# The gated half's LayerNorm as two fused VectorE steps, its splits moved into the gate's projection

## Chip, cores and metric

The kernel runs on one core of one Trainium2 chip. The metric is the device time of one execution in microseconds (us). The time before is 1013.77 us, the median of 3 runs (1012.42 to 1014.16).

## What is computed

One layer of a streaming encoder on x with 512 tokens of 1024 channels. The part that matters here is the token mixer: three branches read the same modulated input h, each is projected to 1024 channels, and the three are merged by sigmoid gates. The change lies in the third branch, a spatial gate.

```python
def _sgu(uv, g_sg, b_sg, w_s, b_s):
    uv = jax.nn.gelu(uv, approximate=False)
    u, v = jnp.split(uv, 2, axis=-1)
    v = _layer_norm(v) * g_sg + b_sg            # over the 1024 channels of a token
    v = v.reshape(B, nb, SG_BLOCK, SG_GROUPS, SG_GW)      # blocks of 128 tokens, 8 groups of 128 channels
    z = jnp.einsum('gts,bnsgc->bntgc', ws, v) + b_s[:, :, None]
    return u * z.reshape(B, S, SG_WIDTH)

    merged = gates[:, :, 0] * y_a + gates[:, :, 1] * y_b + gates[:, :, 2] * y_c
    return merged @ w_o
```

Six rows of modulation (shift, scale and gate for each sub-layer) come from a product of the condition vector with w_ada. After the mixer come a residual LayerNorm, a gated MLP with a short convolution, and a second LayerNorm.

## The kernel before

All matrix products are made from f32 data split in two: a high part (rounded to the type that TensorE takes, a copy on ScalarE) and a low part (value minus high part, on VectorE). `mm3` issues three matmuls for each product. Weights come in chunks of 128 x 1024: `load` brings one from memory on SyncE's queue (3 buffers), `wsplit` makes the high part on ScalarE (L90) and the low part on VectorE (L91), with two buffers for each part. `chunk` takes the chunks in the order of a written plan and splits one chunk ahead of use.

The 512 tokens are four tiles (TT = 4) of 128. The stage around the change runs in this order:

- `uv_half(2)` and `uv_half(3)` project the two halves of v (512 channels each). A half takes four weight chunks (q = 0 to 3) of 24 matmuls, and at its end a Gelu on ScalarE (L803) writes one tile for each token tile: `v0[t]` and `v1[t]`. `uv_half` can take a hook, called after each chunk.
- Four row tiles are loaded: `gsg` and `bsg`, gain and offset of v's LayerNorm, in two halves, each copied to all partitions.
- Eight merges of the second branch (m = 0 to 7): a gate (for m = 4 to 7 projected here by 24 matmuls and put through tanh at L278; the first four were made earlier), a projection of 24 matmuls (`py`), its product with the gate on VectorE (L295) and the sum on GpSimd (L298, POOL in the profile). Beside each merge runs `ada_piece(1, m)`: two loads `adar` of w_ada and two accumulations on VectorE (L678, L680). The LayerNorm of v (`v_norm`) stands beside merges 0 to 3, a whole token tile each: statistics on VectorE, inverse root on GpSimd (`power`: L113, L116; L125 makes the shift), scale and shift on VectorE (L816), gain on VectorE (L819), offset on GpSimd (L820). The splits of the normalised v (`v_split`, L829 and L830), two groups of channels each, stand beside merges 4 to 7. `ada_cols` then turns the accumulated row into columns (`pmc`).
- `sg_weights`, then `uv_half(0)` and `uv_half(1)` project u; beside the second, `z_step` makes the spatial products, which read v's splits.
- Three more groups of modulation accumulate in the same way (`ada_piece(2, m)` belongs to the merges of the third branch).

The program's lines give an order of precedence, but a planner fixes the order of instructions on each engine when the kernel is built, from its own costs and from when inputs and buffers are ready in its model. An instruction can therefore be issued ahead of lines above it. On the chip each engine then runs its list in order. Tiles with one tag share a fixed number of buffers: `pt` has eight, and holds `gsg`, `bsg`, the row tiles of the first residual gate (`gttb`), the two accumulators of a modulation row and its loads `adar`; `act` has 48.

Of the kernel before, what the change touches and what calls it, by code (L numbers as in the profile page):

```python
# [8 lines left out]
F32 = mybir.dt.float32  # L9
# [3 lines left out]
ALU = mybir.AluOpType  # L13
AX = mybir.AxisListType

P = 128
# [3 lines left out]
TT = 4  # L20
# [6 lines left out]
LN_EPS = 1e-5  # L27
# [23 lines left out]
def trunk(ctx: ExitStack, tc: tile.TileContext, A, out):  # L51
    nc = tc.nc

    const = ctx.enter_context(tc.tile_pool(name="const", bufs=1))
    sb = ctx.enter_context(tc.tile_pool(name="sb", bufs=1))
    wp = ctx.enter_context(tc.tile_pool(name="wp", bufs=2))
    sm = ctx.enter_context(tc.tile_pool(name="sm", bufs=4))
    pp = ctx.enter_context(tc.tile_pool(name="pp", bufs=8, space=bass.MemoryType.PSUM))

    def ps(name):  # L60
        return pp.tile([P, 512], F32, name=name, tag="ps")

    def act_t(name, dt=F32R):
        return sb.tile([P, 512], dt, name=name, tag="act", bufs=48)
# [13 lines left out]
    def f(ap):  # L78
        return ap.bitcast(F32)
# [16 lines left out]
    def mm3(o, wh, wl, xh, xl, start, stop):  # L96
        nc.tensor.matmul(o, wh, xl, start=start, stop=False)  # L97
        nc.tensor.matmul(o, wl, xh, start=False, stop=False)  # L98
        nc.tensor.matmul(o, wh, xh, start=False, stop=stop)  # L99
# [11 lines left out]
    def power(dst, src, scale, eps, n):  # L111
        t = sm.tile([P, 8], F32, name="pw", tag="pw")
        nc.gpsimd.tensor_scalar(  # L113
            out=t[:, :n], in0=src, scalar1=scale, scalar2=eps, op0=ALU.mult, op1=ALU.add
        )
        nc.gpsimd.tensor_tensor(out=dst, in0=t[:, :n], in1=neghalf[:, :n], op=ALU.pow)  # L116
# [3 lines left out]
    def ln_finish(st):  # L120
        mv = sm.tile([P, 2], F32, name="mv", tag="mv")
        a = nc.vector.bn_aggr(out=mv, in_=st.rearrange("p a b -> p (a b)"))  # L122
        rs = sm.tile([P, 2], F32, name="rs", tag="rs")
        power(rs[:, 0:1], mv[:, 1:2], 1.0, LN_EPS, 1)
        b = nc.gpsimd.tensor_scalar(  # L125
            out=rs[:, 1:2], in0=mv[:, 0:1], scalar1=rs[:, 0:1], scalar2=-1.0, op0=ALU.mult, op1=ALU.mult
        )
        last[:] = [a.ins, b.ins]
        return rs

    def ln_stats(halves):
        st = sm.tile([P, 2, 6], F32, name="st", tag="st")
        for i, hv in enumerate(halves):
            nc.vector.bn_stats(out=st[:, i, :], in_=hv)
        return ln_finish(st)

    def row_tiles(r, alloc, name):
        ts = []
        for n in range(2):
            t = alloc(f"{name}{n}", F32)  # L140
            nc.sync.dma_start(
                out=t, in_=A["rows"][r : r + 1, n * 512 : (n + 1) * 512].broadcast_to([P, 512])
            )
            ts.append(t)
        return ts
# [4 lines left out]
    for t in range(TT):  # L150
        for n in range(2):
            nc.sync.dma_start(
                out=xs[t][n], in_=A["x"][t * P : (t + 1) * P, n * 512 : (n + 1) * 512]
# [85 lines left out]
    def chunk(key):  # L239
        if key not in plan:  # L240
            return wsplit(A[key[0]][key[1:]], D, key[0])
        i = used[0]
        assert plan[i] == key
        for j in (i, i + 1):
            if j < len(plan) and j not in split:
                split[j] = wsplit(A[plan[j][0]][plan[j][1:]], D, plan[j][0])
        used[0] += 1
        return split[i]
# [21 lines left out]
    def gate(b, m, pg=None):  # L270
        if pg is None:
            gh, gl = chunk(("wg", b * KT + m))
            pg = ps("pg")
            for k in range(KT):
                c = slice(k * P, (k + 1) * P)
                mm3(pg, gh[:, c], gl[:, c], hT_hi[k], hT_lo[k], k == 0, k == KT - 1)
        th = act_t(f"th{b}{m}", F32)
        nc.scalar.activation(th, pg, AF.Tanh, scale=0.5)  # L278
        return th
# [3 lines left out]
    def merge(b, m, bh, bl, th):  # L283
        yh, yl = chunk(("wb", b * KT + m))
        py = ps("py")
        for k in range(KT):
            c = slice(k * P, (k + 1) * P)
            mm3(py, yh[:, c], yl[:, c], bh[k], bl[k], k == 0, k == KT - 1)
        if b == 0:
            merged[m] = m_t(f"mg{m}")  # L290
            nc.vector.scalar_tensor_tensor(
                out=merged[m], in0=th, scalar=1.0, in1=py, op0=ALU.add, op1=ALU.mult
            )
        else:
            nc.vector.scalar_tensor_tensor(  # L295
                out=th, in0=th, scalar=1.0, in1=py, op0=ALU.add, op1=ALU.mult
            )
            nc.gpsimd.tensor_tensor(out=merged[m], in0=merged[m], in1=th, op=ALU.add)  # L298
# [80 lines left out]
    with tc.issue_after(md_done[4]):  # L379
# [7 lines left out]
        for t in range(TT):  # L387
            nc.vector.tensor_scalar_mul(
                out=ang[:, t, :], in0=kst[:, K_FREQ : K_FREQ + 32], scalar1=posf[:, t : t + 1]
            )  # L390
        kq = const.tile([P, TT, 32], F32, name="kq")
        for step in (COARSE, 1.0):
            nc.vector.tensor_scalar(
                out=kq, in0=ang, scalar1=INV_2PI, scalar2=MAGIC * step, op0=ALU.mult, op1=ALU.add
            )
            nc.vector.tensor_scalar_add(out=kq, in0=kq, scalar1=-MAGIC * step)
            for c2 in TWO_PI:
                nc.vector.scalar_tensor_tensor(
                    out=ang, in0=kq, scalar=-c2, in1=ang, op0=ALU.mult, op1=ALU.add
                )  # L400
        nc.vector.tensor_scalar(
            out=ang, in0=ang, scalar1=3.1415925, scalar2=-3.1415925, op0=ALU.min, op1=ALU.max
# [3 lines left out]
            out=kq, in0=ang, scalar=-1.0, in1=ang, op0=ALU.mult, op1=ALU.max  # L406
        )
        nc.vector.tensor_scalar(
            out=kq, in0=kq, scalar1=-1.0, scalar2=1.5707963267948966, op0=ALU.mult, op1=ALU.add
# [12 lines left out]
    for t in range(TT):  # L422
# [14 lines left out]
            out=tA, in0=src, in1=cosT[:, t : t + 1, :].broadcast_to([P, 2, 32]), op=ALU.mult  # L437
        )
        nc.vector.tensor_tensor(
            out=tB, in0=src, in1=sinT[:, t : t + 1, :].broadcast_to([P, 2, 32]), op=ALU.mult  # L440
# [331 lines left out]
    for g in range(4):  # L772
        if g % 2 == 0:
            wh, wl = chunk(("wpool", g // 2))
        for mo in range(2):
            m = 2 * g + mo
# [12 lines left out]
    def uv_half(i, nm, hook=None):  # L789
        tiles = [act_t(f"{nm}{i}{t}", F32) for t in range(TT)]  # L790
        pu = [ps("pu") for _ in range(TT)]
        for q in range(4):
            wh, wl = chunk(("wsg", i, q))
            for t in range(TT):
                ts_ = slice(t * P, (t + 1) * P)
                for kk in range(2):
                    k = 2 * q + kk
                    c = slice(kk * 512, (kk + 1) * 512)
                    mm3(pu[t], hT_hi[k][:, ts_], hT_lo[k][:, ts_], wh[:, c], wl[:, c], k == 0, k == KT - 1)
            if hook:  # L800
                hook(q)
        for t in range(TT):
            nc.scalar.activation(tiles[t], pu[t], AF.Gelu)  # L803
        return tiles

    v0 = uv_half(2, "v")
    v1 = uv_half(3, "v")
    gsg = row_tiles(6, pt_t, "gsg")
    bsg = row_tiles(7, pt_t, "bsg")
    vn_hi = []  # L810
    vn_lo = []

    def v_norm(t):
        rs = ln_stats([v0[t], v1[t]])
        for n, vt in enumerate((v0[t], v1[t])):
            nc.vector.tensor_scalar(  # L816
                out=vt, in0=vt, scalar1=rs[:, 0:1], scalar2=rs[:, 1:2], op0=ALU.mult, op1=ALU.add
            )
            nc.vector.tensor_tensor(out=vt, in0=vt, in1=gsg[n], op=ALU.mult)  # L819
            nc.gpsimd.tensor_tensor(out=vt, in0=vt, in1=bsg[n], op=ALU.add)  # L820

    def v_split(g):
        vh = act_t(f"vnh{g}")
        vl = act_t(f"vnl{g}")
        r = slice((g % 4) * P, (g % 4 + 1) * P)
        vv = (v0, v1)[g // 4]
        for t in range(TT):
            ts_ = slice(t * P, (t + 1) * P)
            nc.scalar.copy(out=vh[:, ts_], in_=vv[t][:, r])  # L829
            nc.vector.tensor_tensor(  # L830
                out=vl[:, ts_], in0=vv[t][:, r], in1=f(vh[:, ts_]), op=ALU.subtract
            )
        vn_hi.append(vh)
        vn_lo.append(vl)

    for m in range(KT):
        th = th1[m] if m < len(th1) else gate(1, m)
        merge(1, m, mx_hi, mx_lo, th)
        ada_piece(1, m)
        if m < 4:  # L840
            v_norm(m)
        else:
            v_split(2 * m - 8)
            v_split(2 * m - 7)
    shf = ada_cols(1, C_SHF, False, "shf")


# [47 lines left out]
    def z_step(i, uu):  # L895
        if i > 0:
            z_transpose(2 * i - 2)
            z_transpose(2 * i - 1)
        if uu is not None:
            z_product(2 * i, uu)  # L900
            z_product(2 * i + 1, uu)

    u0 = uv_half(0, "u")
    u1 = uv_half(1, "u", lambda q: z_step(q, u0) if q < 2 else None)
    th2 = {0: gate(2, 0)}
    z_step(2, u1)
# [7 lines left out]
    for m in range(KT):  # L914
# [5 lines left out]
            out=ml, in0=merged[m], scalar=0.5, in1=f(mh), op0=ALU.mult, op1=ALU.subtract  # L920
# [248 lines left out]
    for i in range(NP):  # L1169
        half = []  # L1170
        for v in range(2):
            m = 2 * i + v
# [4 lines left out]
            else:  # L1177
# [7 lines left out]
            t = pt_t("zc")  # L1185
# [4 lines left out]
                out=t[:, 1:512], in0=pz[:, 0:511], scalar=cols[:, cc + 1 : cc + 2],  # L1190
                in1=t[:, 1:512], op0=ALU.mult, op1=ALU.add,
            )
            nc.vector.scalar_tensor_tensor(  # L1193
                out=t[:, 2:512], in0=pz[:, 0:510], scalar=cols[:, cc : cc + 1],
                in1=t[:, 2:512], op0=ALU.mult, op1=ALU.add,
# [152 lines left out]
```

## Time and profile before

| | |
|---|---|
| median of 3 runs | 1013.77 us (1012.42 to 1014.16) |
| profiled execution, its own time | 1013.85 us |
| span of the profiled execution | 1012.1 us |
| mean granted TensorE clock | 0.986 |
| data moved | 119.20 MB, mean 118 GB/s |

The page of the profile gives busy time for each engine: PE is TensorE's matmuls, PEld its weight loads, DVE VectorE, ACT ScalarE, POOL GpSimd and SP SyncE, whose queue issues the loads. A row of a group of instructions gives line, engine, operation, output<-inputs, shape and count, then busy us and mean ns, then idle time in front of it and who ended it. A row of a timeline gives start and duration in us, then the same names; `x2` is two instructions merged into one row, and the bracket is the idle time of that engine before it and who ended it. A row of a table of windows gives the window, its length, busy time and count for each engine, the granted TensorE clock, the share of the DMA engines and GB/s. Times are counted from the start of the span.

### The profile page before, as it was taken

To read this page: it belongs to the slowest core of one execution; us is meant where nothing else is said; L and a number is where in the kernel's file an instruction comes from. 1 tells how busy PE (TensorE), PEld (TensorE's weight loads), DVE (VectorE), ACT (ScalarE), POOL (GpSimd) and SP (SyncE) were. 2 spreads that over 40 slices of the span, in tenths; PEclk is the share of its full clock that TensorE was granted. 3 is DMA by queue.
4 is the path that set the end of the run, shared out by engine and by line. 5 is a ranking of instruction groups with operands and counts; after the bars stand their busy time and mean duration, and the time that the engine had idled before them with its cause. 6 is when DMAs were issued, how large, how long until landed. Compare 5 with 4: busy or idle time off the path is not lost.

```text
span 1012.1 us, 12192 instructions
## 1 busy us (share of the span) xinstructions
PE 966.5 (95%) x4496; PEld 799.8 (79%) x4496; DVE 609.5 (60%) x931; ACT 384.0 (38%) x650; POOL 326.2 (32%) x341
## 2 busy tenths in 40 slices
PE   4889999999999998999999998999999999999996
PEld 3778888877888867788888876998888888778885
DVE  8957655558445398754434378776666675633267
ACT  3355555442324322332332233654444444421221
POOL 6555110212350072110001666411111121466564
PEclk9899999999999998999999999999999999999999
DMA  9612111137333327652222364124333343243322
GB/s 343 255 30 85 65 50 50 58 124 234 101 96 112 105 63 241 203 159 84 84 84 91 97 189 165 43 63 145 119 112 125 115 136 103 85 146 85 103 84 83
DMA packets 45276, 119.20 MB, mean 118 GB/s; under 512 B 5280, under 2 KB 8736, under 8 KB 45216
## 3 DMA queue, kind: packets, MB, share of 16 engines
q1 hardware_dynamic: 45072, 118.30, 36.6%
q8 instruction: 35, 0.57, 0.2%
q14 instruction: 25, 0.20, 0.1%
q10 hardware_dynamic: 144, 0.12, 0.0%
HBM read 116.30 MB, written 2.10 MB: 117 GB/s over the span
## 4 chain that ended last, share of the span: by engine, by line
PE 69%; DVE 11%; DMA 9%; POOL 4%; issue 4%; ACT 2%; SPq 0%; DVEq 0%; POOLq 0%; ACTq 0%
PE pzu L97 7%; PE pzu L99 7%; PE pzu L98 7%; PE pyd L97 4%; PE pyd L98 4%; PE pyd L99 4%; PE pg L98 3%; PE pg L99 3%; PE pg L97 3%; DMA adar<-in_ada 3%; PE pu L97 3%; PE pu L98 3%; PE pu L99 3%; PE py L98 2%; PE py L99 2%
## 5 line engine op out<-in xcount | busy, mean ns | idle before, releaser
L1204 POOL TENSOR_TENSOR zc<-zc 128x512 f32<-128x512 f32 x22 | 32.8, 1489 | 178.9 <-ACT zc L1203 178.9
L937 POOL TENSOR_TENSOR d<-d,gtfb 128x512 f32<-128x512 f32 x44 | 71.6, 1651 | 43.5 <-DMA d<-in_wdn 36.8
L298 POOL TENSOR_TENSOR mg<-mg,th 128x512 f32<-128x512 f32 x16 | 27.0, 1687 | 140.7 <-DVE th L295 121.5
L1189 DVE SCALAR_TENSOR_TENSOR zc<-pzu,cols,zc 128x511 f32<-128x511 f32 x44 | 32.8, 747 | 52.0 <-ACT zc L1186 52.0
L680 DVE SCALAR_TENSOR_TENSOR ada<-adar,cact,ada 128x512 f32<-128x512 f32 x56 | 52.5, 964 | 15.1 <-DMA adar<-in_ada 15.1
L1186 ACT ACTIVATE zc<-pzu,cols 128x512 f32<-128x512 f32 x44 | 34.2, 779 | 71.9 <-PE pzu L99 71.9
L942 DVE TENSOR_TENSOR dl<-d,dh 128x1024 fp32r<-128x1024 f32 x18 | 29.2, 1625 | 52.8 <-ACT dh L941 52.8
L90 ACT CAST wbh<-wb 128x1024 fp32r<-128x1024 f32 x24 | 25.2, 1050 | 65.7 <-PE py L99 57.3
L91 DVE TENSOR_TENSOR wgl<-wg,wgh 128x1024 fp32r<-128x1024 f32 x22 | 27.3, 1242 | 36.6 <-ACT wgh L90 35.5
L91 DVE TENSOR_TENSOR wupl<-wup,wuph 128x1024 fp32r<-128x1024 f32 x38 | 46.8, 1233 | 0.0
L91 DVE TENSOR_TENSOR wbl<-wb,wbh 128x1024 fp32r<-128x1024 f32 x24 | 33.9, 1412 | 16.3 <-ACT wbh L90 16.1
L91 DVE TENSOR_TENSOR wsgl<-wsg,wsgh 128x1024 fp32r<-128x1024 f32 x16 | 19.6, 1223 | 39.4 <-ACT wsgh L90 39.4
L941 ACT CAST dh<-d 128x1024 fp32r<-128x1024 f32 x18 | 18.8, 1047 | 60.7 <-PE pyd L99 60.6
L90 ACT CAST wuph<-wup 128x1024 fp32r<-128x1024 f32 x38 | 39.5, 1039 | 0.0
L278 ACT ACTIVATE th<-pg 128x512 f32<-128x512 f32 x22 | 13.1, 597 | 63.1 <-PE pg L99 63.1
L113 POOL TENSOR_SCALAR pw<-mv 128x1 f32<-128x1 f32 x20 | 8.3, 413 | 82.5 <-DVE mv L122 69.5
L90 ACT CAST wsgh<-wsg 128x1024 fp32r<-128x1024 f32 x16 | 16.8, 1049 | 47.2 <-PE pu L99 45.1
L1193 DVE SCALAR_TENSOR_TENSOR zc<-pzu,cols,zc 128x510 f32<-128x510 f32 x44 | 32.7, 747 | 1.3
L937 POOL TENSOR_TENSOR o<-o,gttb 128x512 f32<-128x512 f32 x16 | 25.4, 1616 | 17.3 <-DMA o<-in_wo 17.3
L201 DVE SCALAR_TENSOR_TENSOR acc<-ada,cact,acc 128x256 f32<-128x256 f32 x48 | 29.7, 678 | 0.0
L735 POOL TENSOR_TENSOR asum<-apad 128x527 f32<-128x527 f32 x8 | 9.2, 1147 | 59.5 <-ACT apad L730 25.9
L601 POOL TENSOR_SCALAR pe<-pe,mx 128x128 f32<-128x128 f32 (+3 forms) x32 | 16.8, 533 | 35.8 <-DVE mx L600 26.4
(1370 smaller groups left out, 3230.7 us busy)
## 6 DMA issues: line engine op xcount, KB each, us to landing
wup<-in_wup SPq DMA_DIRECT2D x44, 512.0 KB, 3.6
adar<-in_ada SPq DMA_DIRECT2D x64, 256.0 KB, 3.9
wb<-in_wb SPq DMA_DIRECT2D x24, 512.0 KB, 3.6
wg<-in_wg SPq DMA_DIRECT2D x22, 512.0 KB, 3.6
d<-in_wdn SPq DMA_DIRECT2D x22, 512.0 KB, 3.6
ada<-in_ada SPq DMA_DIRECT2D x32, 256.0 KB, 5.0
wsg<-in_wsg SPq DMA_DIRECT2D x16, 512.0 KB, 3.6
wa<-in_wa SPq DMA_DIRECT2D x8, 512.0 KB, 3.6
```

Of the source, the lines that this page charges most:

```text
L90: nc.scalar.copy(out=hi[:, :n], in_=raw[:, :n])
L91: nc.vector.tensor_tensor(out=lo[:, :n], in0=raw[:, :n], in1=f(hi[:, :n]), op=ALU.subtract)
L97: nc.tensor.matmul(o, wh, xl, start=start, stop=False)
L98: nc.tensor.matmul(o, wl, xh, start=False, stop=False)
L99: nc.tensor.matmul(o, wh, xh, start=False, stop=stop)
L201: nc.vector.scalar_tensor_tensor(out=acc[i], in0=src, scalar=cact[:, k : k + 1], in1=acc[i], op0=ALU.mult, op1=ALU.add,)
L680: nc.vector.scalar_tensor_tensor(out=acc[n], in0=src, scalar=cact[:, k : k + 1], in1=acc[n], op0=ALU.mult, op1=ALU.add,)
L937: nc.gpsimd.tensor_tensor(out=raw[:, c], in0=raw[:, c], in1=gt[n], op=ALU.mult)
L1186: nc.scalar.activation(t, pz, AF.Identity, bias=cols[:, cc + 3 : cc + 4], scale=cols[:, cc + 2 : cc + 3])
L1189: nc.vector.scalar_tensor_tensor(out=t[:, 1:512], in0=pz[:, 0:511], scalar=cols[:, cc + 1 : cc + 2], in1=t[:, 1:512], op0=ALU.mult, op1=AL ...
L1193: nc.vector.scalar_tensor_tensor(out=t[:, 2:512], in0=pz[:, 0:510], scalar=cols[:, cc : cc + 1], in1=t[:, 2:512], op0=ALU.mult, op1=ALU.add,)
L1204: nc.gpsimd.tensor_tensor(out=val, in0=val, in1=gate, op=ALU.mult)
```

## The change

The LayerNorm of v is written as two fused VectorE steps for each half tile: (v - mean) * gain, then (that) * inverse root + offset. The statistics of all four token tiles and one inverse root over the four are made in `v_stats`, at merge 0. Each of the eight merges then takes half a token tile: merges 0 to 3 the first half of tiles 0 to 3, merges 4 to 7 the second half. The GpSimd offset step (L820) and shift step (L125) are gone. The splits move from merges 4 to 7 into the first u projection, two groups after each of its four weight chunks.

```diff
-    def v_norm(t):
-        rs = ln_stats([v0[t], v1[t]])
-        for n, vt in enumerate((v0[t], v1[t])):
-            nc.vector.tensor_scalar(
-                out=vt, in0=vt, scalar1=rs[:, 0:1], scalar2=rs[:, 1:2], op0=ALU.mult, op1=ALU.add
-            )
-            nc.vector.tensor_tensor(out=vt, in0=vt, in1=gsg[n], op=ALU.mult)
-            nc.gpsimd.tensor_tensor(out=vt, in0=vt, in1=bsg[n], op=ALU.add)
+    mvv = const.tile([P, TT, 2], F32, name="mvv")
+    rsv = const.tile([P, TT], F32, name="rsv")
+
+    def v_stats():
+        for t in range(TT):
+            st = sm.tile([P, 2, 6], F32, name="st", tag="st")
+            for n, vt in enumerate((v0[t], v1[t])):
+                nc.vector.bn_stats(out=st[:, n, :], in_=vt)
+            nc.vector.bn_aggr(out=mvv[:, t, :], in_=st.rearrange("p a b -> p (a b)"))
+        power(rsv, mvv[:, :, 1], 1.0, LN_EPS, TT)
+
+    def v_norm(t, n):
+        vt = (v0, v1)[n][t]
+        nc.vector.scalar_tensor_tensor(
+            out=vt, in0=vt, scalar=mvv[:, t, 0:1], in1=gsg[n], op0=ALU.subtract, op1=ALU.mult
+        )
+        nc.vector.scalar_tensor_tensor(
+            out=vt, in0=vt, scalar=rsv[:, t : t + 1], in1=bsg[n], op0=ALU.mult, op1=ALU.add
+        )
...
         merge(1, m, mx_hi, mx_lo, th)
         ada_piece(1, m)
-        if m < 4:
-            v_norm(m)
-        else:
-            v_split(2 * m - 8)
-            v_split(2 * m - 7)
+        if m == 0:
+            v_stats()
+        v_norm(m % 4, m // 4)
...
-    u0 = uv_half(0, "u")
+    def both_splits(q):
+        v_split(2 * q)
+        v_split(2 * q + 1)
+
+    u0 = uv_half(0, "u", both_splits)
```

## The prediction

> **What bounds the kernel now.** I read the page first, then a table of windows with one stretch for each merge of the second branch, then TensorE's waits in it, then the VectorE and ScalarE rows in front of each wait.
>
> ```profile
> PE 966.5 (95%) x4496; PEld 799.8 (79%) x4496; DVE 609.5 (60%) x931; ACT 384.0 (38%) x650; POOL 326.2 (32%) x341
> PE 69%; DVE 11%; DMA 9%; POOL 4%; issue 4%; ACT 2%; SPq 0%; DVEq 0%; POOLq 0%; ACTq 0%
> ```
>
> TensorE is busy 95% of the span and holds 69% of the chain that ended last, so an edit of VectorE work pays only where TensorE waits for VectorE. The edited code lies in one such place: the eight merges of the second branch (m = 0 to 7; 4 to 7 have a gate projection in front) and the u projection behind them.
>
> ```profile
> core 0: us, PE busy (x) PEld busy (x) DVE busy (x) ACT busy (x) POOL busy (x), PEclk, DMA share, GB/s
> 359.40:365.00 5.60, 5.60 (x25) 4.49 (x24) 5.60 (x9) 1.53 (x2) 4.48 (x5) 1.00 0.03 8
> 365.00:371.10 6.10, 5.88 (x25) 4.43 (x24) 6.01 (x8) 1.05 (x1) 5.20 (x7) 1.00 0.31 86
> 371.10:377.20 6.10, 5.89 (x26) 4.43 (x24) 5.25 (x6) 1.05 (x1) 6.10 (x6) 1.00 0.28 86
> 377.20:386.50 9.30, 7.35 (x25) 5.57 (x24) 9.30 (x9) 1.04 (x1) 6.15 (x4) 0.82 0.62 172
> 386.50:397.60 11.10, 11.10 (x49) 8.92 (x48) 7.01 (x11) 4.19 (x11) 1.29 (x1) 1.00 0.83 271
> 397.60:413.00 15.40, 12.59 (x49) 9.88 (x48) 12.77 (x25) 4.18 (x11) 2.20 (x1) 0.89 0.68 209
> 413.00:424.10 11.10, 11.10 (x50) 9.03 (x49) 6.90 (x14) 4.18 (x11) 1.29 (x1) 1.00 0.60 195
> 424.10:438.00 13.90, 13.25 (x66) 10.74 (x64) 11.16 (x19) 6.23 (x14) 2.80 (x2) 1.00 0.64 190
> 438.00:459.90 21.90, 21.90 (x97) 18.13 (x98) 8.85 (x17) 4.99 (x7) 2.28 (x1) 1.00 0.46 143
> ```
>
> An undisturbed merge takes 5.60 us (first row), an undisturbed gate and merge 11.10 (fifth and seventh). Merges 1 and 2 lose 0.5 each, merge 3 loses 9.30 - 5.60 = 3.7, gate 5 with merge 5 loses 15.40 - 11.10 = 4.3, and the last row has 13.90 - 13.25 = 0.65 of idle TensorE. Sum 9.65 us. In the rows of 3.7 and 4.3 the granted clock falls to 0.82 and 0.89 behind the wait, so a long wait costs more than its own length. The last row, the u projection of the first half, has no TensorE wait, and VectorE is busy for only 8.85 of its 21.90 us.
>
> ```profile
> 365.63 0.50 PE L98 MATMUL py<-mx0h,wbl 128*128 128x512 f32 x1 [0.22 <-DVE wbl L91]
> 371.70 0.50 PE L98 MATMUL py<-mx0h,wbl 128*128 128x512 f32 x1 [0.20 <-DVE wbl L91]
> 379.51 0.60 PE L98 MATMUL py<-mx0h,wbl 128*128 128x512 f32 x1 [1.95 <-DVE wbl L91]
> 400.83 0.80 PE L98 MATMUL pg<-hT0h,wgl 128*128 128x512 f32 x1 [2.81 <-DVE wgl L91]
> 425.17 0.50 PE L98 MATMUL pg<-hT0h,wgl 128*128 128x512 f32 x1 [0.65 <-DVE wgl L91]
> ```
>
> All five waits are for the low part of a weight chunk, made on VectorE at L91. What stood in front of it:
>
> ```profile
> 371.30 1.05 ACT L90 CAST wbh<-wb 128x1024 fp32r<-128x1024 f32 x1 [5.05 <-PE py L99]
> 392.70 1.04 ACT L90 CAST wgh<-wg 128x1024 fp32r<-128x1024 f32 x1
> ...
> 375.39 2.93 DVE L816 TENSOR_SCALAR v<-v,rs 128x512 f32<-128x512 f32 x2 [0.85 <-POOL rs L125]
> 378.25 1.21 DVE L91 TENSOR_TENSOR wbl<-wb,wbh 128x1024 fp32r<-128x1024 f32 x1
> 379.38 1.28 DVE L819 TENSOR_TENSOR v<-v,gsg 128x512 f32<-128x512 f32 x2
> 397.31 0.75 DVE L680 SCALAR_TENSOR_TENSOR ada<-adar,cact,ada 128x512 f32<-128x512 f32 x1 [2.56 <-DMA adar<-in_ada]
> 398.89 0.75 DVE L680 SCALAR_TENSOR_TENSOR ada<-adar,cact,ada 128x512 f32<-128x512 f32 x1 [0.82 <-DMA adar<-in_ada]
> 399.55 1.22 DVE L91 TENSOR_TENSOR wgl<-wg,wgh 128x1024 fp32r<-128x1024 f32 x1
> ```
>
> Two kinds of stall. In merges 1 to 3 it is the norm: merge 3's low part has its high part ready at 371.30 + 1.05 = 372.35 and starts at 378.25, behind two scale-and-shift steps of 2.93 us that themselves waited for POOL's statistic. In gate 5 it is the modulation: the high part is ready at 392.70 + 1.04 = 393.74, the low part starts at 399.55, behind two accumulations that wait 2.56 and 0.82 us for their DMA. The 0.65 us at 425.17 is a gate's as well, and I count it here. So 0.5 + 0.5 + 3.7 = 4.7 us belong to the norm and 4.3 + 0.65 = 4.95 us to the modulation.
>
> **The change part by part.**
>
> ```profile
> L816 DVE TENSOR_SCALAR v<-v,rs 128x512 f32<-128x512 f32 x8 | 8.9, 1144 | 1.1 <-POOL rs L125 1.0
> L819 DVE TENSOR_TENSOR v<-v,gsg 128x512 f32<-128x512 f32 x8 | 6.3, 814 | 0.0
> L816 DVE TENSOR_SCALAR v<-v,rs x8: 535/1498/1519, 358.6 to 376.8; 128x512 f32<-128x512 f32 x8
> L819 DVE TENSOR_TENSOR v<-v,gsg x8: 672/678/1775, 360.2 to 380.0; 128x512 f32<-128x512 f32 x8
> L820 POOL TENSOR_TENSOR v<-v,bsg 128x512 f32<-128x512 f32 x8 | 12.0, 1514 | 3.0 <-DVE v L819 3.0
> L116 POOL TENSOR_TENSOR rs<-pw,neghalf 128x1 f32<-128x1 f32 x4 | 3.1, 785 | 0.2
> L1229 DVE SCALAR_TENSOR_TENSOR out<-out,mv,lnfg 128x512 f32<-128x512 f32 x8 | 5.7, 748 | 0.1
> L1241 DVE SCALAR_TENSOR_TENSOR out<-out,rs,lnfb 128x512 f32<-128x512 f32 x4 | 3.0, 748 | 0.4 <-POOL rs L116 0.4
> L829 ACT CAST vnh<-v x32: 292/297/303, 393.6 to 433.6; 128x128 fp32r<-128x128 f32 x32
> L830 DVE TENSOR_TENSOR vnl<-v,vnh x32: 279/283/288, 400.7 to 439.2; 128x128 fp32r<-128x128 f32 x32
> 359.61 0.60 ACT L803 ACTIVATE v<-pu 128x512 f32<-128x512 f32 x1 [0.76 <-PE pu L99]
> ```
>
> (1) The norm's own work. Before: 8.9 + 6.3 = 15.2 us of VectorE and 12.0 us of POOL. After: 16 fused steps, and the kernel already holds both forms at the same size and type in its final LayerNorm, L1229 and L1241, at 748 ns. 16 x 0.748 = 12.0 us of VectorE, none of POOL. Less work by 3.2 us on VectorE, in windows where VectorE is 86 to 100% busy (5.25 of 6.10, 9.30 of 9.30).
>
> Against it stands the minimum of L816, 535 ns. The median is 1498, and pairs like that at 375.39 (2.93 for two) ran while POOL was adding L820. I take the mean, 1144, since those adds are part of the same norm and always run against it. The Trainium skill, "VectorE: DVE Perf Modes", section on the perf-mode tier table, says that an f32 one-tensor operation from SBUF can run at double rate and a two-tensor one cannot, which speaks against the change: each half tile gives up one fast form. What that would make of the time, from rows, is the fifth rival.
>
> A fused step can still be slowed by the merge's own add on POOL, about one in 5.6 us. I allow 0.4 us of TensorE loss in merges 1 to 3 for that and for a fused step that starts just ahead of a weight's low part. The cover is about 3 us: the high part is ready 1.25 us into a merge (372.35 against 371.10), the low part takes 1.21, the merge 5.60, and 5.60 - 1.25 - 1.21 = 3.1.
>
> (2) The statistics. One power over four tiles replaces four, so L116 runs once for four times, and L125 goes. A wait is added: the first fused step now needs the last tile's Gelu (359.61 + 0.60 = 360.21), its statistic and POOL's power (L116, 0.785), so the norm begins near 362.3, an estimate that gives all of these 2 us, instead of at 358.6. What is queued behind it on VectorE is the low part for merge 1, needed at 365.0 and ready at about 361: nothing else is late. Then no step waits for POOL again.
>
> (3) Where the halves land. The order on an engine goes by readiness more than by the program's line: the last pair of L816 stands behind merge 3 in the program, whose matmuls end at 386.5, and yet all eight started by 376.8. I therefore expect the 16 steps to run nearly back to back, first halves done by about 362.3 + 8 x 0.75 + two low parts and a merge step (1.21 + 1.21 + 0.7) = 371, second halves by about 378, not one pair a merge.
>
> (4) The modulation's transfers are not edited but move, since gsg and bsg share eight buffers with them:
>
> ```profile
> 305.26 0.33 SPq L676 DMA_DIRECT2D adar<-in_ada  x1
> 380.69 2.89 SPq L676 DMA_DIRECT2D adar<-in_ada  x4
> 403.33 1.79 SPq L676 DMA_DIRECT2D adar<-in_ada  x2
> 431.56 4.62 SPq L676 DMA_DIRECT2D adar<-in_ada  x3
> ```
>
> SyncE issues none from 305.26 until 380.69, just when the last gsg step (379.38 + 1.28 = 380.66) ends. In the change gsg and bsg of the first half come free at about 371, the second half's at about 378. So the run of loads starts some 10 us earlier, first with two buffers, then with four. With four buffers, 380.69 to 400, transfers ran at up to 271 GB/s and the accumulations fell behind; with two, from 403.33 to 436.2, 15 loads took 2.2 us each, and cost at most the 0.65. Some of the loads that ran with four buffers will run with two, so the loss should shrink, but the loads meet weight chunks in another place. Bounds: from nothing lost (gain 4.95) to the rival's loss below. I take 4.0 of the 4.95 as staying, nearest to the rows before, since the same loads go through the same queue.
>
> (5) The splits. They take 32 x 0.297 = 9.5 us of ScalarE and 32 x 0.283 = 9.1 us of VectorE out of merges 4 to 7 and put them beside the u projection, where the 438.00 row shows 21.90 - 8.85 = 13.0 us of idle VectorE and 21.90 - 4.99 = 16.9 of idle ScalarE. They issue no DMA and nothing on POOL or SyncE, so no queue is passed there. Cost nothing while that cover holds; without it, see the third rival. The first spatial product needs them only behind the u projection's first half.
>
> Sum: 4.7 - 0.4 + (4.95 - 4.0) = 5.25 us gained. The profiled execution took 1013.85 (span 1012.1), within 0.1 of the median 1013.77, so the forecast is 1013.8 - 5.3 = 1008.5, with 1006 to 1011 as its own range.
>
> **The rivals.**
>
> First, slower: the earlier loads stall the gateless merges. For: between 371 and 385 each low part has only those 3 us of cover, a load in a two-buffer run takes 2.2 us, and VectorE executes in order. If the order puts four accumulations in front of each low part, 4 x 2.2 = 8.8 us pass in a merge of 5.6: 3.2 us in each of merges 1 to 3, 9.6 less the cover of 3 is 6.6, and 1.7 for the clock (merge 3 lost 3.7 against 1.95 waited). With 4.7 gained: 1013.8 - 4.7 + 8.3 = 1017.4. It decides from three accumulations a merge on (6.6 us against 5.6). Against: the run with two buffers had about three per weight chunk from 405 on and lost 0.65.
>
> Second, no change: the norm's stall goes and the four-buffer run, now partly in merges without a gate, loses as much again: 1013.8 - 4.7 + 4.5 = 1013.6.
>
> Third, the splits come in blocks in front of the u chunks. A block of eight costs ScalarE 2.4 and VectorE 2.3 us, hidden by a chunk's slack of about 3; all 32 in one block would delay a chunk by 9.5 - 3 = 6.5. Then 1008.5 + 6.5 = 1015.0. Against: the 16.9 us of idle ScalarE, and readiness order.
>
> Fourth, larger gain: the modulation's waits go as well, because the loads are spread or because the second half's steps really stay one a merge and keep the run at two buffers: 1013.8 - 9.65 = 1004.2.
>
> Fifth, the fused form is the dearer one, because POOL's adds are not what slowed L816: 2 x 0.748 against 0.535 + 0.678, the undisturbed times of L816 and L819, is 0.283 us a half tile, or 8 x 0.283 = 2.3 on a full VectorE: 1013.8 + 2.3 = 1016.1. The median of L816 speaks against it. It is the outcome by the tier table named above.
>
> Sixth, the change does not do what it says: the halves run in one block. That is part of the forecast, and costs nothing by itself.
>
> **How the numbers follow.** Forecast 0.50; slower by the first 0.18; no change 0.10; blocks 0.04; larger gain 0.14; fused form 0.04. A measurement of this kernel can tell about 0.2%, or 2 us, from no change. Faster: 0.50 + 0.14 = 0.64; same 0.10, and 0.01 of the blocks, 0.11; slower 0.18 + 0.04 + 0.03 = 0.25. The range leaves out about a tenth at either end: 1003.5, a little under the larger gain, to 1016.5, above the fused form and most ways into the first rival.
>
> **What would show it.** Right: L816, L819 and L820 gone, sixteen fused steps near 0.75 us and done before 380; the waits at 365, 371 and 379 gone; modulation loads resuming near 371; the first u stretch without a TensorE wait though its VectorE busy time rises to about 16 us. The step on the modulation is right if gate 5's wait, or one like it in merges 2 to 5, stays near 3 us. Wrong: fused steps near 1.5 us; a low part in merges 1 to 3 behind an accumulation that waits for its DMA; TensorE waits between 438 and 460; TensorE waits far from this stage, which nothing above would explain.

## The result, and the profile after

The changed kernel takes 1012.41 us (median of 20 runs, 1008.63 to 1015.96), the kernel before 1012.42 us (20 runs, 1008.97 to 1015.52). The ratio is 1.0005, 95% interval 0.9994 to 1.0015: no change. The profiled execution took 1015.96 us, span 1014.3; it lies at the upper end of its runs, so I compare its stage with the stage before and not its total.

The eight merges, from the first product of merge 0 to the first u product, took 78.54 us before and take 80.18 us after (360.08 to 440.26). The windows of the changed kernel, cut at the same places as before (merges 2 and 3 in one row):

```profile
core 0: us, PE busy (x) PEld busy (x) DVE busy (x) ACT busy (x) POOL busy (x), PEclk, DMA share, GB/s
360.10:365.70 5.60, 5.60 (x26) 4.49 (x25) 5.44 (x11) 1.53 (x2) 2.41 (x2) 1.00 0.03 9
365.70:371.30 5.60, 5.60 (x26) 4.47 (x24) 5.60 (x9) 1.05 (x1) 1.16 (x2) 1.00 0.46 140
371.30:387.10 15.80, 13.28 (x50) 10.06 (x48) 13.15 (x16) 2.09 (x2) 5.10 (x3) 0.89 0.68 216
387.10:399.90 12.80, 11.34 (x50) 8.92 (x48) 8.21 (x11) 2.58 (x3) 2.30 (x2) 1.00 0.70 226
399.90:414.10 14.20, 11.59 (x50) 8.84 (x48) 7.42 (x10) 2.58 (x3) 1.28 (x1) 1.00 0.60 185
414.10:426.50 12.40, 11.31 (x49) 8.92 (x48) 7.65 (x11) 2.58 (x3) 2.20 (x1) 1.00 0.59 190
426.50:440.30 13.80, 13.09 (x66) 10.68 (x64) 9.78 (x23) 8.18 (x26) 2.35 (x2) 1.00 0.59 183
440.30:462.10 21.80, 21.80 (x97) 18.07 (x98) 9.84 (x24) 7.75 (x19) 2.09 (x1) 1.00 0.34 102
```

Merge 1 is clean now. Merges 2 and 3 together lose 15.80 - 11.20 = 4.6 us, as much as merges 1 to 3 lost before (4.7). The four gates with their merges lose 1.7, 3.1, 1.3 and 0.7 us, 6.8 in all, against 4.95 before. The u projection, with the splits in it, has no wait. TensorE's waits in the same stage:

```profile
372.58 0.50 PE L97 MATMUL py<-mx0l,wbh 128*128 128x512 f32 x1 [0.90 <-ACT wbh L90]
374.70 0.51 PE L98 MATMUL py<-mx0h,wbl 128*128 128x512 f32 x1 [1.62 <-DVE wbl L91]
388.93 0.50 PE L98 MATMUL pg<-hT0h,wgl 128*128 128x512 f32 x1 [1.46 <-DVE wgl L91]
401.61 0.50 PE L98 MATMUL pg<-hT0h,wgl 128*128 128x512 f32 x1 [1.35 <-DVE wgl L91]
408.61 0.50 PE L98 MATMUL py<-mx0h,wbl 128*128 128x512 f32 x1 [1.26 <-DVE wbl L91]
415.56 0.50 PE L98 MATMUL pg<-hT0h,wgl 128*128 128x512 f32 x1 [1.09 <-DVE wgl L91]
427.61 0.50 PE L98 MATMUL pg<-hT0h,wgl 128*128 128x512 f32 x1 [0.71 <-DVE wgl L91]
```

And the timeline of ScalarE (first row), VectorE and SyncE's queue (last row) ahead of two of them:

```profile
365.88 1.05 ACT L90 CAST wbh<-wb 128x1024 fp32r<-128x1024 f32 x1 [4.07 <-PE py L99]
...
364.78 2.07 DVE L826 SCALAR_TENSOR_TENSOR v<-v,mvv,gsg 128x512 f32<-128x512 f32 x3
366.77 3.40 DVE L829 SCALAR_TENSOR_TENSOR v<-v,rsv,bsg 128x512 f32<-128x512 f32 x5
370.08 0.69 DVE L295 SCALAR_TENSOR_TENSOR th<-th,py 128x512 f32<-128x512 f32 x1
370.68 0.75 DVE L829 SCALAR_TENSOR_TENSOR v<-v,rsv,bsg 128x512 f32<-128x512 f32 x1
371.34 1.50 DVE L678 TENSOR_SCALAR ada<-adar,cact 128x512 f32<-128x512 f32 x1
372.77 0.74 DVE L829 SCALAR_TENSOR_TENSOR v<-v,rsv,bsg 128x512 f32<-128x512 f32 x1
373.43 1.21 DVE L91 TENSOR_TENSOR wbl<-wb,wbh 128x1024 fp32r<-128x1024 f32 x1
...
399.94 0.49 DVE L678 TENSOR_SCALAR ada<-adar,cact 128x512 f32<-128x512 f32 x1 [3.92 <-DMA adar<-in_ada]
400.34 1.22 DVE L91 TENSOR_TENSOR wgl<-wg,wgh 128x1024 fp32r<-128x1024 f32 x1
...
366.88 6.98 SPq L676 DMA_DIRECT2D adar<-in_ada  x3
```

The high part for merge 2 is ready at 366.93 (365.88 + 1.05), its low part starts at 373.43: in between stand seven fused steps, the product of merge 0 and the first accumulation, without a gap. The two waits of 0.90 and 1.62 us are one stall: merge 2's second product needs this low part, and the planner has put merge 3's first product in between, which itself waits 0.90 us for merge 3's high part. The norm no longer waits for POOL and no longer runs at 1.5 us a step; it stands in the way as a block. Gate 5 has the same picture as before: an accumulation that waits 3.92 us for its load, and the low part behind it. The loads resumed at 366.88, 14 us earlier than before.

That accumulation at 399.94 (L678, the form that begins a row) does not belong to the row of this stage. Of the 30 modulation loads issued here, before as after, 14 are for the second row; the planner has then gone on with the 16 of the third row, whose columns are made only from 576 on (L707). The last four of the five modulation waits stand behind accumulations of the third row, which this stage does not need. The fused steps themselves, as groups:

```profile
L826 DVE SCALAR_TENSOR_TENSOR v<-v,mvv,gsg x8: 702/746/751, 358.0 to 366.1; 128x512 f32<-128x512 f32 x8
L829 DVE SCALAR_TENSOR_TENSOR v<-v,rsv,bsg x8: 739/751/753, 366.8 to 374.6; 128x512 f32<-128x512 f32 x8
```

### The profile page after: what moved, and what is told of

The parts are those of the page before. It is cut to its first block, busy times and chain, and to the rows that moved or that the text cites. A ratio compares the mean times of both kernels' runs of the same rounds, so it can differ in the third digit from the quotient of the medians.

```text
span 1014.3 us, 12171 instructions
## 1 busy us (share of the span) xinstructions
PE 966.4 (95%) x4496; PEld 799.5 (79%) x4496; DVE 604.3 (60%) x931; ACT 384.2 (38%) x650; POOL 310.4 (31%) x323
## 4 chain that ended last, share of the span: by engine, by line
PE 70%; DVE 10%; DMA 9%; POOL 4%; issue 4%; ACT 2%; SPq 0%; DVEq 0%; POOLq 0%; ACTq 0%
PE pzu L97 7%; PE pzu L98 7%; PE pzu L99 7%; PE pyd L97 4%; PE pyd L99 4%; PE pyd L98 4%; DMA adar<-in_ada 3%; PE pg L98 3%; PE pg L99 3%; PE pg L97 3%; PE pu L97 3%; PE pu L99 3%; PE pu L98 3%; PE py L98 2%; PE py L99 2%
## 5 line engine op out<-in xcount | busy, mean ns | idle before, releaser
L680 DVE SCALAR_TENSOR_TENSOR ada<-adar,cact,ada 128x512 f32<-128x512 f32 x56 | 51.5, 954 | 17.7 <-DMA adar<-in_ada 17.7
L90 ACT CAST wgh<-wg 128x1024 fp32r<-128x1024 f32 x22 | 23.1, 1052 | 17.1 <-DMA adar<-in_ada 9.4
```

Of the source, the lines that this page charges most:

```text
L90: nc.scalar.copy(out=hi[:, :n], in_=raw[:, :n])
L680: nc.vector.scalar_tensor_tensor(out=acc[n], in0=src, scalar=cact[:, k : k + 1], in1=acc[n], op0=ALU.mult, op1=ALU.add,)
```

## The experiments

All runs are against the kernel before on the same chip; "ratio" is to it, with its 95% interval. Added lines shift the line numbers in some runs: L680 and L816 can stand as L682 or L683 and as L819 there.

My theory after the result: two stalls add up, the block of fused steps and the modulation loads, and the loads reach the merges only because gsg and bsg hold their buffers. Rival A: each load costs the same wherever it runs, because VectorE takes its list in order. Rival B: the splits or the fused steps are too dear.

**Taking the buffers apart, and one half tile a merge.** Four runs. Rows apart in the changed kernel:

```diff
+    gsg = row_tiles(6, act_t, "gsg")
+    bsg = row_tiles(7, act_t, "bsg")
     v0 = uv_half(2, "v")
     v1 = uv_half(3, "v")
-    gsg = row_tiles(6, pt_t, "gsg")
-    bsg = row_tiles(7, pt_t, "bsg")
```

> The changed kernel, with gsg and bsg moved out of the eight shared buffers into others and loaded ahead of the v projections, so that the modulation loads no longer wait for the norm. Theory (two stalls, joined by the buffers): the modulation accumulations run beside the v projections, where VectorE is idle; the gate waits of 1.46, 1.35, 1.26, 1.09 and 0.71 us go, the wait of merge 2 behind the block of fused steps (0.90 + 1.62 and the clock, some 4.6 us) stays. Time 5 to 7 us below the kernel before, ratio near 0.994. Rival A (the loads cost the same wherever they run, since VectorE waits for them in order): as many waits appear in the v projections, time within 2 us of before. Rival B (the moved splits and dearer fused steps eat the gain): waits between 440 and 462, time within 2 us of before.

One half tile a merge (`products` keeps the instruction of L295 for each merge; `issue_after` queues what follows behind it on its engine):

```diff
-        v_norm(m % 4, m // 4)
+        with tc.issue_after(products[1, m]):
+            v_norm(m % 4, m // 4)
```

> The changed kernel, with each pair of fused steps queued on VectorE behind the product of its own merge, so that it really is one half tile a merge. Theory: the wait in merge 2 (some 4.6 us with the clock) goes, no low part stands behind a block of fused steps; gsg and bsg are held to merges 3 and 7, so the modulation loads resume near 380 with two buffers for the first row, and the waits for them stay, 3 to 7 us in all. Time 2 to 5 us below before, ratio 0.995 to 0.998. Rival B (the fused steps themselves are too dear): merges 1 to 3 still lose 4 us, no gain.

Both edits:

> Both edits: gsg and bsg in other buffers, and one pair of fused steps behind the product of its merge. Theory: both stalls go, the eight merges take near 68.4 us instead of 78.5; time 8 to 11 us below before, ratio near 0.991. Rival A: the loads stall the v projections instead, 3 us below before or less. Rival B: waits in merges 1 to 3 or between 440 and 462, 5 us below or less.

The first edit alone, in the kernel before:

> The kernel before, with only gsg and bsg moved out of the shared buffers and loaded ahead of the v projections. Theory: the modulation's share of the loss, 4.95 us, goes, the norm's share of 4.7 us stays in merges 1 to 3: time 4 to 5 us below before, ratio near 0.9955. If the change's norm were worth nothing by itself this equals the run with the rows apart in the changed kernel; if it were worth the 4.7 us that the prediction gave it, that run lies 4 us below this one. Rival A: no gain.

Measured: rows apart 1017.64 us, ratio 1.005 (1.003 to 1.0069); one a merge 1008.88, 0.9962 (0.9945 to 0.9979); both 1012.91, 1.0003 (0.9992 to 1.0014); before with rows apart 1015.64, 1.0028 (1.0012 to 1.0043). TensorE's waits with the rows apart, in the v projections and in merge 2, and VectorE's rows in front of the third of them:

```profile
331.79 0.50 PE L97 MATMUL pu<-wsgl,hT4h 128*128 128x512 f32 x1 [1.45 <-DVE wsgl L91]
338.48 0.50 PE L97 MATMUL pu<-wsgl,hT6h 128*128 128x512 f32 x1 [0.92 <-DVE wsgl L91]
346.11 0.50 PE L97 MATMUL pu<-wsgl,hT0h 128*128 128x512 f32 x1 [1.87 <-DVE wsgl L91]
383.82 0.50 PE L98 MATMUL py<-mx0h,wbl 128*128 128x512 f32 x1 [1.22 <-DVE wbl L91]
...
344.17 0.75 DVE L680 SCALAR_TENSOR_TENSOR ada<-adar,cact,ada 128x512 f32<-128x512 f32 x1 [3.40 <-DMA adar<-in_ada]
344.83 1.22 DVE L91 TENSOR_TENSOR wsgl<-wsg,wsgh 128x1024 fp32r<-128x1024 f32 x1
```

The waits of the gates are gone, as the theory had it, and have come up again ahead of the stage, beside the first branch's merges and in the v projections, where VectorE was half idle. Rival A is right here: an idle engine is no cover when the accumulation stands at the head of its list and waits for its load. So the theory's second half, that the shared buffers are to blame, falls; the three runs with the rows apart, expected 4 to 11 us below the kernel before, came out level with it or slower.

Its first half holds. With the rows apart in both, the block in merge 2 (1.005) against one a merge (1.0003) is 0.0047, or 4.7 us; the profile of the latter has no wait in any merge of the second branch. By the same measure the norm of the kernel before (1.0028) costs 2.5 us against one a merge. Both figures are rough, since the waits ahead of the stage, from 266 to 347, differ between these runs as well (8.25 us in sum with one a merge, 7.0 and 6.1 in the other two). With the rows where they were, one a merge leaves these waits of the loads, and gains 3.5 us:

```profile
405.62 0.50 PE L98 MATMUL pg<-hT0h,wgl 128*128 128x512 f32 x1 [1.62 <-DVE wgl L91]
412.00 0.50 PE L98 MATMUL py<-mx0h,wbl 128*128 128x512 f32 x1 [0.61 <-DVE wbl L91]
420.15 0.50 PE L98 MATMUL pg<-hT0h,wgl 128*128 128x512 f32 x1 [2.30 <-DVE wgl L91]
```

**The parts alone.** Only the splits moved (the norm of the kernel before, `both_splits` as the hook), and only the fused norm, which is this edit of the changed kernel:

```diff
-        v_norm(m % 4, m // 4)
+        if m < 4:
+            v_norm(m, 0)
+            v_norm(m, 1)
+        else:
+            v_split(2 * m - 8)
+            v_split(2 * m - 7)
...
-    u0 = uv_half(0, "u", both_splits)
+    u0 = uv_half(0, "u")
```

> The kernel before, with only the splits moved into the u projection. Theory (the splits are hidden in both places; what stalls gate 5 is the wait for a DMA at the head of VectorE's list, not VectorE's work): norm waits of 0.22, 0.20 and 1.95 us as before, modulation waits of 3 to 5 us somewhere in merges 4 to 7, no wait between 440 and 462: within 2 us of before, ratio 0.998 to 1.002. Rival B (the splits crowd the u projection): waits there, 3 us or more above before. Rival C (9 us less VectorE work in merges 4 to 7 frees the low parts): modulation waits gone, 4 to 5 us below before.

> Only the fused norm with its common statistics: a whole tile beside each of merges 0 to 3 in the program, splits beside merges 4 to 7 as before. Theory (the planner runs the sixteen fused steps in one block whichever merge they are written beside, in front of merge 2's low part): a wait of 2 to 3 us and a clock drop in merge 2, the modulation loads resume near 367 as in the changed kernel: within 2 us of before and of the changed kernel. Rival C (the order by halves is what hurt): no wait in merge 2, 4 us below before.

Measured: splits only 1014.99 us, ratio 1.0023 (1.0008 to 1.0039); fused only 1013.39, 1.0009 (0.9995 to 1.0023). TensorE's waits with the splits moved, in merge 3 and in the u projection:

```profile
378.67 0.50 PE L98 MATMUL py<-mx0h,wbl 128*128 128x512 f32 x1 [1.95 <-DVE wbl L91]
446.21 0.50 PE L97 MATMUL pu<-wsgl,hT2h 128*128 128x512 f32 x1 [1.87 <-DVE wsgl L91]
```

and with the fused norm alone, in merge 2:

```profile
371.95 0.66 PE L98 MATMUL py<-mx0h,wbl 128*128 128x512 f32 x1 [1.60 <-DVE wbl L91]
```

Fused alone behaves as the changed kernel: the block runs in front of merge 2's low part whichever merges the steps are written beside. My expectation for the splits was missed: they cost 1.87 us in the u projection in that run, and the modulation waits (1.65, 2.69 and 1.71 us in gates and merges 4 to 7) were larger in sum, 6.05 against 3.46 before, not smaller. Taking 9 us of VectorE work out of merges 4 to 7 freed nothing there.

**Pacing the accumulations.** If the fault is an accumulation that waits at the head of the list, queueing it behind the weights' low parts should end it. First, each pair behind the product of its own merge, in the changed kernel and in the run with both edits:

```diff
+            with tc.issue_after(products[idx, k]) if (idx, k) in products else ExitStack():
                 if k == 0:
                     nc.vector.tensor_scalar_mul(out=acc[n], in0=src, scalar1=cact[:, 0:1])
```

> The changed kernel, with each pair of modulation accumulations queued on VectorE behind the product of its own merge (first, second and third branch), so that none can stand in front of low parts while its load is on the way. Theory: the five modulation waits (5.9 us of idle TensorE, 6.85 lost) go, merge 2's stall of some 4.6 us behind the block of fused steps stays: 5 to 7 us below before, ratio near 0.994. Rival A (the loads cost TensorE as much wherever they are accumulated): no gain.

> The run with the rows apart and one half tile a merge, and with each pair of accumulations queued behind the product of its merge. Theory: neither stall is left in the merges, and the loads, issued ahead and accumulated one pair a merge, do not stall the first branch or the v projections (1.06 to 1.98 us each there in the earlier runs): 8 to 11 us below before, ratio near 0.991. Rival A: waits of a microsecond and more for low parts stay somewhere from 220 to 440, 4 us below before or less.

Measured: 1025.18 us, ratio 1.0121 (1.0099 to 1.0143), and 1016.21, 1.0028 (1.0011 to 1.0044). Both expectations were missed by time. The modulation waits in the gates and merges of the second branch are gone in both, and merge 2 kept its 0.90 and 1.61 us in the first, as expected; but a row now ends behind the last product, just where it is read. TensorE's two longest waits for it in the first run (`adal` is the low part of the first row, `ada` the third row's accumulator):

```profile
307.03 0.79 PE L702 MATMUL pgt<-adal,onesr 128*128 128x512 f32 x1 [4.36 <-POOL adal L697]
593.28 1.87 PE L711 MATMUL pmc<-ones,ada 128*128 128x1 f32 x8 [6.77 <-DVE ada L684]
```

So the pace was right and the place was late. With two merges of lead, and the first row left alone:

```diff
-            with tc.issue_after(products[idx, k]) if (idx, k) in products else ExitStack():
+            with tc.issue_after(products[idx, k - 2]) if (idx, k - 2) in products else ExitStack():
```

> The rows apart, one half tile a merge, and the accumulation pairs of the second and third modulation rows queued behind the product of the merge two before their own, so that the row is complete before it is read; the first row's pairs are left as in the kernel before. Theory: no wait for a low part from 220 to 440, none at the end of the first row (4.36 us in the paced run) and little at the end of the others (1.62 and 5.68 there): 7 to 11 us below before, ratio near 0.991. Rival A (each load costs TensorE about the same wherever it is accumulated): other waits of the same sum appear, within 3 us of before.

> The changed kernel with one half tile a merge (gsg and bsg still in the shared buffers), and the accumulation pairs of the second and third rows queued behind the product of the merge two before their own. Theory: the three waits left in the run with one half tile a merge (1.62, 0.61, 2.30 us) shrink; but the loads start only when the rows come free in merges 3 and 7, so the second row may end late and be waited for at its read: 3 to 8 us below before. Rival A: as that run, 3.5 us below before, or worse.

Measured: with the rows apart 1005.93 us, ratio 0.9926 (0.9912 to 0.994), 7.5 us below before and faster than both kernels; with the rows in the shared buffers 1010.44, 0.9976 (0.9963 to 0.999), with waits of 1.66 and 2.08 us left at two gates. Some windows of the former, merges 2 and 3, one gate with its merge, the last one, and the sum over the stage:

```profile
370.50:376.10 5.60, 5.60 (x26) 4.49 (x25) 5.50 (x7) 1.05 (x1) 1.72 (x1) 1.00 0.64 189
376.10:381.70 5.60, 5.60 (x26) 4.49 (x25) 5.50 (x7) 1.05 (x1) 1.72 (x1) 1.00 0.65 189
392.80:403.90 11.10, 11.10 (x50) 9.03 (x49) 7.23 (x8) 2.59 (x3) 1.73 (x1) 1.00 0.46 138
415.00:427.60 12.60, 12.60 (x65) 10.57 (x64) 9.52 (x22) 8.14 (x25) 3.15 (x2) 1.00 0.51 151
sum 68.30, PE 68.30 PEld 55.62 DVE 51.02 ACT 20.59 POOL 15.72; mean PE 8.54 PEld 6.95 DVE 6.38 ACT 2.57 POOL 1.97
```

TensorE is busy for all of the 68.30 us, 10.2 less than before. The total gained 7.5, so some 2.7 us are lost again behind the stage; one wait there that the kernel before does not have is 1.28 us at 584.35, for a low part (L966). VectorE is still 98% busy in merges 2 and 3 (5.50 of 5.60), and nothing waits for it: how full it is did not matter, what stands in front of a low part did. The pacing does two things at once, though: most of the third row's accumulations move out to the third branch, so that 16 accumulations and not 30 stand in this stage, and the paced ones that stay no longer wait for their loads. The share of each was not separated.

**What the change is worth without its order.** The norm of the kernel before, a whole tile behind the product of its own merge, first alone, then with the rows apart and the accumulations paced two merges ahead:

```diff
         if m < 4:
-            v_norm(m)
+            with tc.issue_after(products[1, m]):
+                v_norm(m)
```

> The kernel before, its norm unfused, a whole tile queued on VectorE behind the product of its own merge (statistics too). It tells whether the gain of 3.5 us with one half tile a merge comes from the order or from the fused steps. Theory (what counts is that no low part stands behind a run of norm steps): the wait of 1.95 us in merge 3 goes, but a whole tile with POOL adding takes about 2 x (1.5 + 0.7) = 4.4 us, more than the cover of 3, so waits of 0.5 to 2 us stay in merges 3 to 5: 0 to 3 us below before. If order alone were enough: 3.5 us below, as with the fused steps. If the fused steps are what gains: as before or slower.

> The kernel before with everything of the fastest run but the change itself: rows apart, accumulation pairs two merges behind, the norm unfused, a whole tile behind the product of its own merge in merges 0 to 3, splits in merges 4 to 7. It tells what the fused steps, the halves and the moved splits are worth when no order stands against them. Theory (the order carried the gain, and a whole unfused tile of some 4.4 us is more than the cover of 3): waits of up to 2 us in merges 2 to 5, so 4 to 7 us below before, 1 to 4 us above the fastest run. If the change is worth nothing even then: as the fastest run, ratio near 0.9926. If it is worth what the prediction gave it: 3 us or less below before.

Measured: ordered alone 1009.92 us, ratio 0.9964 (0.9949 to 0.9979); with all of it 1014.55, 1.0023 (1.0006 to 1.0039). Both miss my expectation: the first gained a little more than the 0 to 3 us forecast, the second lost 2 to 3 where 4 to 7 of gain were forecast. TensorE's waits with the order alone, at two gates:

```profile
394.88 0.50 PE L98 MATMUL pg<-hT0h,wgl 128*128 128x512 f32 x1 [1.63 <-DVE wgl L91]
409.03 0.50 PE L98 MATMUL pg<-hT0h,wgl 128*128 128x512 f32 x1 [2.19 <-DVE wgl L91]
```

and TensorE's largest wait with all of it, at merge 5, with some of the VectorE rows in front of its low part:

```profile
404.27 0.79 PE L98 MATMUL py<-mx0h,wbl 128*128 128x512 f32 x1 [4.94 <-DVE wbl L91]
...
395.79 2.06 DVE L819 TENSOR_SCALAR v<-v,rs 128x512 f32<-128x512 f32 x2
400.06 2.41 DVE L683 SCALAR_TENSOR_TENSOR ada<-adar,cact,ada 128x512 f32<-128x512 f32 x2
402.40 0.68 DVE L822 TENSOR_TENSOR v<-v,gsg 128x512 f32<-128x512 f32 x1
403.00 1.21 DVE L91 TENSOR_TENSOR wbl<-wb,wbh 128x1024 fp32r<-128x1024 f32 x1
```

Of the two waits with the order alone only the second stands behind a load (an accumulation at 407.09 that waits 2.02 us); the first is the norm's own, since the low part made at 393.61 stands behind a scale-and-shift step that waits 1.94 us for POOL's statistic. The order alone still gains as much without the fused steps (0.9964) as with the whole change (0.9962): while the loads still stall the gates, the fused form, the halves and the moved splits are worth nothing that can be measured. With the loads out of the way they are worth 1.0023 - 0.9926 = 0.0097, nearly 10 us, and the stage takes 78.0 us (357.42 to 435.42) instead of 68.3. There the unfused norm runs on to 403.08, the gain step (L822) just ahead of merge 5's low part, among splits and accumulations that wait for no load. Which of the three parts carries this was not separated.

## Why the prediction was right or wrong

The measured time lies inside the range; the forecast of a gain clear of noise does not hold, and the second rival's number (1013.6, no change) was nearest, though not by its mechanism: it had the norm's stall gone, and it only moved. That the time falls into the range is luck, since the range was wide enough for two terms of the sum that were too small by 4.2 and 2.8 us.

**The work (step 1).** Right in size: 746 and 751 ns against the 748 taken from L1229 and L1241, and POOL's adds gone. The VectorE total of the norm moved from 15.2 to 11.2 us (5.6 for each line) and TensorE lost as much in merges 1 to 3, so the dearness of the fused form decided nothing here. The rule of the tier table that I weighed against the row, "VectorE: DVE Perf Modes" of the Trainium skill, agrees with the trace in direction only: undisturbed, L816 with one tensor took 0.535 us and L819 with two 0.678, where the table's f32 column, for 2048 elements, has a factor of about two; the fused form, at 0.75, is not in the table.

**The statistics (step 2).** Misread, at no cost to the sum. The first fused step needs only its own tile's mean and began at 358.0, not 362.3; only the second needs the inverse root, which POOL made in 1.71 + 1.40 us for the four tiles (L113, L116), done at 366.41. So all first steps ran ahead of all second ones, and the second steps began at 366.77, just when merge 2's low part could have been made.

**The 0.4 us for merges 1 to 3: the step that failed.** It came out at 4.6. Step 3 said that sixteen steps would run nearly back to back from 362 to 378, and step 1 worked out a cover of 3 us, yet the loss was sized for a single fused step ahead of a low part. The sixth rival even named the block and said that it costs nothing by itself. The prediction held both numbers and did not put them together: a cover of 3.1 us is four fused steps, and in a block of sixteen, with low parts somewhere among them, more than four can stand in front of one. Seven did, with two other steps, 6.5 us. It also read the cause of the norm's stall as the slow steps and POOL's statistic. The runs show that the place decides more: with the same fused steps, one pair a merge removes it, and the old steps in the same place gain as much, though one wait for POOL's statistic then stalls gate 5.

**The modulation (step 4).** Right that the loads resume earlier and that the loss stays; the size was low. I kept 4.0 us of 4.95, and 6.8 were lost, in five waits of 0.71 to 1.46 us and not in one of 2.81. That the loss comes from VectorE waiting for a load at the head of its list is shown by the rows in front of the low parts (3.92 us at 399.94) and by pacing: with two merges of lead the waits are gone. What the prediction did not see is that about half of these loads serve the third row. The first rival, loads stalling the gateless merges, did not come: merges 2 and 3 were stalled by the norm.

**The splits (step 5).** Right for the changed kernel, which has no wait from 440.3 to 462.1; not safe in general, since the splits alone met a wait of 1.87 us there. They ran as blocks of 20 and 12 casts, which the third rival named, and not where the edit put them: the 20 on ScalarE, and 14 of the 32 low parts on VectorE, ran ahead of 440.3 beside merge 7, so VectorE's busy time in the first u stretch rose from 8.85 to 9.84 us and not to about 16.

**The sum.** 4.7 - 0.4 + 0.95 = 5.25 us of gain became 0.1 - 1.85 = -1.75; the stage is 1.64 longer in the profiled pair, and over 20 runs each the difference is nil.

## What to carry to other kernels

Where engines run their lists in order, look at what stands in front of the operation that the busiest engine waits for, not at the total of work on that list: removing work from a full engine gained nothing here until the order was set, and then the engine could stay 98% full in two merges at no cost. An operation that waits for a load should be queued behind the operations that others wait for, with some lead before its own reader. Look also whether the operations that wait are needed in that stage at all. When a prediction says that steps will run as a block, compare the block's length with the cover in the same line.

## What the runs showed of the hardware

A wait of about 2 us was followed by a lower granted clock in some profiled executions and not in others. Merge 3 of the kernel before waited 1.95 us and its window had a clock of 0.82; with the splits moved the same wait, 1.95 us at 378.67, was followed by a full clock, as this window shows:

```profile
377.00:383.00 6.00, 4.33 (x19) 3.52 (x20) 6.00 (x7) 0.57 (x1) 3.90 (x4) 1.00 0.53 153
```

Waits up to 1.46 us in the changed kernel cost no clock in their windows. A stall near 2 us can therefore cost 1.7 us more (3.7 lost against 1.95 waited) or nothing, which is as large as several of the differences told here, and calls for many runs. Each profile is of one execution, so a stage's length in it carries this too.
